# One load of L's diagonal blocks, or four: a change to how the inversion in a gated delta rule layer is fed

## The chip, the cores and the metric

The kernel runs on one core of one Trainium2 chip. The metric is device time in microseconds (us), the median of several executions. Before the change it is 2826.01 us, the median of three runs (2831.53, 2826.01, 2823.58).

## The reference, cut to what matters

Two pre-norm residual layers are computed on 256 tokens of width 2048, in float32. The first mixes tokens by stick-breaking attention, the second by a gated delta rule; each is followed by a SwiGLU feed-forward part. What the change touches is in the second layer, where for each of 32 value heads a lower triangular matrix is inverted:

```
a_mat = where(strict, einsum('nbhcd,nbhsd->nbhcs', k * beta, k) * decay, 0)
t_mat = triangular_solve(a_mat + eye, eye, lower=True, unit_diagonal=True)
u = t_mat @ (v * beta)
w = t_mat @ (k * beta * exp(g))
```

The kernel works with chunks of 128 tokens where the reference has 64, and calls the strictly triangular matrix L.

## The kernel before, in words

**The main stream.** Nearly all the work is products of the 256 tokens with weight matrices, cut into blocks of 512 output columns (`Block`). The weights come from HBM in loads of two row tiles of 128 rows (`load`, 512 KB, the tile `raw`, five buffers; a `qk` block of the delta rule takes two loads of 256 KB for one such tile). `convert` splits each into two float32r parts: ScalarE writes `wh` by a copy (the helper `act`, L190), VectorE writes `wl` by a subtraction (the helper `tt`, L194). TensorE then does 12 products per piece into `acc` (the helper `mm`, L213). Conversions run three pieces ahead (`AHEAD`), and there are four buffers for each of the two parts.

**The side chains.** Everything else (norms, attention, the delta rule) is written as Python generators that the program steps through while it emits the main products. So the order of the instructions on every engine is fixed when the program is built. It is decided by a small model: `self.t` holds a clock for each engine and one for the DMA, `spend` and `transfer` add a cost to them, and `tick` lets a chain go on once its `ready` time has come on the model's TensorE clock and the modelled ScalarE and VectorE clocks are at most `LAG` ahead of it. `transfer` gives each DMA 0.46 us on the issuing queue, then 1.55 us until data flows, its bytes at 360 KB per us, and 0.55 us to land; all DMAs of the model share one line. The DMA clock starts at 0.

**The inversion.** The 32 heads come in eight groups of four. For each group, `gdn_blocks32` writes the 32 x 32 diagonal blocks of L of the four heads and two chunks to a scratch of 32 rows by 1024 in DRAM (eight small DMAs, `scratch<-wide`), and loads the scratch into the tile `lt`, 128 partitions of 4 KB: each quarter of 32 partitions gets the same 128 KB. GpSimd sets the diagonal of `lt` to one (L1003). After that VectorE does 32 steps of forward substitution, two instructions each (`slab<-slab,lt`, L194, and a reduction, L209). The generator yields after some of the steps (`CUT`), so that weight conversions stand between them in VectorE's order. The results go back to a second scratch, and `gdn_inverse` doubles the blocks up to 128 x 128 with products on TensorE.

**Queues.** All these DMAs are issued by SyncE, in program order: a weight load behind the load of `lt` is issued after it. VectorE too executes in order: where an instruction of the substitution waits for `lt`, the conversions behind it wait as well, and TensorE waits for those once it has used up the weights converted ahead.

Of the kernel before, what the change touches and what calls it, by code (L numbers as in the profile page):

```python
# [32 lines left out]
class Slots:  # L33
    """A fixed set of buffers handed out in turn."""
# [13 lines left out]
class Task:  # L48
    """A chain of work that runs between the main matrix products. It yields where its next
    instructions need what it has issued so far; `ready` is when that should be there."""  # L50
# [17 lines left out]
class Operand:  # L68
    """A stationary operand: 128 rows of the contraction for 256 tokens, split into two float32r parts."""
# [8 lines left out]
class Block:  # L78
    """An output block of up to 512 columns: its weights, its stationary operands and what follows it."""
# [8 lines left out]
class Trunk:  # L88
# [10 lines left out]
    LAG = 2.0  # L99
    REST = 8.0  # L100
    GDN_ORDER = [('qk', 0), ('ba',), ('v', 0), ('qk', 1), ('z', 0), ('v', 2), ('v', 1), ('z', 1), ('qk', 2), ('qk', 3), ('v', 3), ('z', 2), ('z', 3), ('out', 0, 4), ('out', 4, 8), ('qk', 4), ('v', 4), ('qk', 5), ('v', 5), ('z', 5), ('z', 4), ('qk', 7), ('v', 6), ('qk', 6), ('out', 8, 16), ('v', 7), ('z', 6), ('z', 7), ('out', 16, 24), ('out', 24, 32)]

    def __init__(self, ctx, tc, ins, out):
        self.tc, self.nc, self.ins, self.out = tc, tc.nc, ins, out
        self.tasks = []
        self.cur = None
        self.table = None
        self.t = {"pe": 0.0, "act": 0.0, "dve": 0.0, "sp": 0.0, "dma": 0.0}
        self.flags = set()
        self.smalls = {}  # L110
        self.persist = ctx.enter_context(tc.tile_pool(name="persist", bufs=1))
        self.wpool = ctx.enter_context(tc.tile_pool(name="weights", bufs=1))
        self.ppool = ctx.enter_context(tc.tile_pool(name="psum", bufs=1, space=PSUM))
        t = self.sb
        self.xs = [t(f"x{n}", [P, NT, NB]) for n in range(4)]
        self.x = [[self.xs[n][:, i, :] for n in range(4)] for i in range(NT)]
        self.hT = []
        for k in range(KT // 2):
            hi, lo = t(f"hTh{k}", [P, 2, S], F32R), t(f"hTl{k}", [P, 2, S], F32R)
            self.hT += [(hi[:, j, :], lo[:, j, :]) for j in range(2)]  # L120
        self.pairs = Slots([(t(f"kh{k}", [P, 2, S], F32R), t(f"kl{k}", [P, 2, S], F32R)) for k in range(self.PAIRS)])
        self.lts = Slots([t("lt", [P, 32, 32])])
        self.slabs = Slots([t(f"slab{k}", [P, NB]) for k in range(self.SLAB)])
        self.gms = Slots([[t(f"gm{k}{hl}", [P, NB], F32R) for hl in range(2)] for k in range(1)])
        self.wide = Slots([t(f"wide{k}", [P, 2, 4, P]) for k in range(self.WIDE)])
        self.acc = [[self.ppool.tile([P, NB], F32, name=f"acc{b}{i}") for i in range(NT)] for b in range(2)]
        self.banks = Slots([self.ppool.tile([P, NB], F32, name=f"bank{k}") for k in range(4)])
        dram = ctx.enter_context(tc.tile_pool(name="scratch", bufs=1, space=bass.MemoryType.DRAM))
        self.scratch = [dram.tile(s, F32, name=f"scratch{k}") for k, s in enumerate(([32, 1024], [8, P * (P + 1)]))]
        self.n = 0  # L130
# [20 lines left out]
    def tick(self, idle=False):  # L151
        """Let the chains go on whose results should be there."""
        ran = False
        for task in list(self.tasks):
            now = self.t["pe"]
            if task.ready <= now and max(self.t["act"], self.t["dve"]) <= now + self.LAG:
                before = dict(self.t)
                self.step(task)
                ran = ran or task.done or before != self.t
        if idle and not ran:  # L160
            later = [task.ready for task in self.tasks if task.ready > self.t["pe"]]
            self.t["pe"] = min(later) if later else self.t["pe"] + 0.1
# [75 lines left out]
    def split(self, hi, lo, src, gain=None):  # L238
        """hi + lo == src (times a gain per partition)."""
        if gain is None:  # L240
            self.act(hi, src)
            self.tt(lo, src, hi.bitcast(F32), ALU.subtract)
        else:
            self.act(hi, src, scale=gain)
            self.stt(lo, src, gain, hi.bitcast(F32), ALU.mult, ALU.subtract)
# [5 lines left out]
    def rsqrt(self, out, in_, scale, eps):  # L251
        """(in * scale + eps) ** -0.5, in place allowed."""
        self.ts(out, in_, scale, ALU.mult, eps, ALU.add)
        self.sync()
        self.act(out, out, AF.Ln)
        self.act(out, out, AF.Exp, scale=-0.5)

# [6 lines left out]
    def constants(self):  # L264
        """What the first products need: the identity and the gains of the mixers' norms, a column to 128 channels."""
        t = self.sb
        self.nc.scalar.preload_act_table_set("natural_log_exp_and_others")
        self.table = 6
        self.ident = t("ident", [P, P])
        self.gains = t("gains", [P, 67])  # L270
        rows = self.slabs.free[0][:32, :P]
        self.nc.scalar.dma_start(rows, self.ins["mix_norm"].rearrange("l (k p) -> (l k) p", p=P))
        make_identity(self.nc, self.ident)
        bank = self.banks.free[0]
        self.tr(bank[:, 0:32], rows)
        self.nc.vector.tensor_copy(self.gains[:, 0:32], bank[:, 0:32])

    def more_constants(self):
        """The other vectors and the masks."""
# [65 lines left out]
    def plan(self, blocks):  # L345
        """Cut blocks into loads of four row tiles and pieces of two."""
# [97 lines left out]
    def load_x(self, n):  # L444
        """Columns n*512.. of x, and the first norm of them."""
# [13 lines left out]
    def norm_begin(self, gain0):  # L459
        """State of one normalisation of x: partial sums and the 16 operands."""  # L460
# [13 lines left out]
    def norm_part(self, st, n):  # L474
        """Transpose columns n*512.. of x into operands."""
# [17 lines left out]
    def norm_stats(self, st, n):  # L493
        """Sum the squares of columns n*512.. of x; the last part gives the scale of each token."""
# [15 lines left out]
        # one Newton step: r * (1.5 - 0.5 * v * r * r)  # L510
# [22 lines left out]
    def pair_operands(self, ops, src, gain=None):  # L533
        """Fill two operands from a [128, 2, 256] source in PSUM."""
# [13 lines left out]
    def transposed_pairs(self, tok, ops, gain=None):  # L548
        """tok: two [128 tokens, 512] slabs -> four operands."""
# [215 lines left out]
    def gdn_gates(self, acc, free):  # L765
        """g = -exp(a_log) * softplus(a + dt_bias), beta = sigmoid(b), per token and head."""
# [42 lines left out]
        # exp of the sum of g over the tokens of chunk 0 after j  # L809
# [15 lines left out]
    def conv(self, jobs):  # L825
        """Causal depthwise convolution over the 256 tokens of channel tiles: (source, result, channel tile)."""
# [31 lines left out]
    def gdn_decay(self, G):  # L858
        """E[j, head, i] = exp of the sum of g over tokens after j up to i: within chunk 0, across, within chunk 1;
        across without the tokens of chunk 0, whose share is in `rest`. For i < j, where nothing looks, it is 1."""  # L860
# [23 lines left out]
    def small(self, name, shape, g):  # L884
        """A small tile, one per three groups in turn."""
        key = (name, g % 3)
        if key not in self.smalls:
            self.smalls[key] = self.sb(f"{name}{g % 3}", shape)
        return self.smalls[key]

    def gdn_scores(self, G):
# [8 lines left out]
        # products of keys with keys and queries: [key token, (k, q), token]  # L900
        m = []
        for j in range(3):
# [10 lines left out]
            # queries see no later keys of their chunk; where L is zero nothing is read  # L913
# [3 lines left out]
        # sums of squares of k and q per token: [token, key head, (k, q), chunk]  # L917
# [29 lines left out]
        # beta / (|k|^2 + eps) and sqrt(|k|^2 + eps)  # L947
# [31 lines left out]
    def gdn_blocks32(self, G):  # L979
        """Inverses of the 32 x 32 diagonal blocks of I + L by forward substitution: partition q * 32 + r holds  # L980
        columns 4q.. and 16 + 4q.. of block r of the eight matrices, and all of the block of L."""
# [18 lines left out]
        self.dma(ltf, bass.AP(tensor=src.tensor, offset=src.offset, ap=[[0, 4], [1024, 32], [1, 1024]]))  # L1000
        yield
        # the diagonal takes the right hand side, which waits negated where the unknown goes
        g.memset(ltf[:, 0:1024:33], 1.0)  # L1003
        for i in range(32):
            n = i + 1
            if i < 16:
                # row i of the left columns and row 16 + i of the right ones
# [23 lines left out]
    def strided(self, a, off, *dims):  # L1031
        """Elements of a [partitions, n] from off on, by (stride, count) per dimension."""
        return bass.AP(tensor=a.tensor, offset=a.offset + off, ap=[list(a.ap[0])] + [[s, n] for s, n in dims])

    def whole(self):
        """Scratch 1 as [128, 8 matrices, 128]."""
        return self.scratch[1][:, :P * P].rearrange("h (j i) -> j h i", i=P)

    def diag(self, at):
        """Rows at.. at + 4 of the 32 x 32 diagonal blocks of the 8 matrices of scratch 1: [32, 4, 32]."""  # L1040
# [3 lines left out]
    def gdn_inverse(self, G, c, a, U):  # L1044
        """U = transpose of (I + L)^-1 for the four heads, by doubling diagonal blocks."""
# [5 lines left out]
        # all but its 32 x 32 diagonal blocks is zero yet: transposed block by block it is transposed  # L1051
# [184 lines left out]
```

## Time and profile before

| | before |
|---|---|
| median of three timed runs | 2826.01 us (2823.58 to 2831.53) |
| span of the profiled execution | 2824.8 us |
| TensorE products busy | 2796.1 us (99% of the span) |
| VectorE busy | 1660.5 us (59%) |
| ScalarE busy | 1363.1 us (48%) |
| GpSimd busy | 11.2 us |
| loads of `lt` | 8, of 512 KB each |

The profile gives no time for the profiled execution beside its span. The stages follow each other in time: attention from 0 to about 420 us, the first feed-forward part to about 1163, the delta rule to about 2063, the second feed-forward part to the end. Products are pipelined and their ends are modelled, so the distance from the start of one to the start of the next says how fast TensorE works; a busy share alone does not.

### The profile page before, as it was taken

How to read it: one execution, taken by the hardware profiler on the slowest of the kernel's cores; microseconds unless marked ns; L12 is line 12 of the kernel's file. 1: busy time of each engine (PE TensorE's matmuls, PEld its weight loads, DVE VectorE, ACT ScalarE, POOL GpSimd, SP SyncE). 2: the span in 40 equal slices, each digit the busy share in tenths (PEclk: the TensorE clock that was granted, in tenths of full speed). 3: DMA queues.
4: the chain of work that ended last, by engine and by line, in shares of the span. 5: the costliest groups of instructions: out<-in, count | busy, mean ns of one | idle time of the engine just before them, and what ended most of it. 6: DMA issues, size and time to landing. Idle time of an engine off the chain costs nothing.

```text
span 2824.8 us, 35294 instructions
## 1 busy us (share of the span) xinstructions
PE 2796.1 (99%) x13290; PEld 2258.6 (80%) x13290; DVE 1660.5 (59%) x2498; ACT 1363.1 (48%) x1896; POOL 11.2 (0%) x95
## 2 busy tenths in 40 slices
PE   8999999999999999999999999999999999999999
PEld 6888888888888888887787788777888888888887
DVE  5555565554454545578777787877654544544544
ACT  5555454434434444565565556545554344344343
POOL 0000000000000000000000000000000000000000
PEclk9999999999999999999999999999999999999999
DMA  6555556566566566555656555545466566566564
GB/s 218 164 160 161 179 165 184 182 191 185 182 188 185 184 187 186 177 165 161 176 145 184 150 158 166 166 140 177 157 181 184 186 185 187 186 185 186 184 186 155
DMA packets 299334, 496.38 MB, mean 176 GB/s; under 512 B 36695, under 2 KB 79002, under 8 KB 299162
## 3 DMA queue, kind: packets, MB, share of 16 engines
q1 hardware_dynamic: 299114, 494.10, 58.0%
q8 instruction: 104, 1.70, 0.3%
q14 instruction: 68, 0.56, 0.1%
q10 hardware_dynamic: 48, 0.02, 0.0%
HBM read 489.33 MB, written 4.72 MB: 175 GB/s over the span
## 4 chain that ended last, share of the span: by engine, by line
PE 92%; DVE 3%; DMA 3%; ACT 1%; issue 1%; SPq 0%; POOL 0%; POOLq 0%; DVEq 0%; ACTq 0%
PE acc L213 85%; PE bank L213 5%; PE bank L222 2%; DMA lt<-scratch 2%; DVE wl L194 1%; DVE slab L194 1%; DVE slab L198 1%; ACT wh L190 0%; ACT slab L190 0%; DVE slab L209 0%; DVE wide L198 0%; DMA x<-in_x_dram 0%; DVE hTl L198 0%; DMA scratch<-wide 0%; SPq L366 0%
## 5 line engine op out<-in xcount | busy, mean ns | idle before, releaser
L194 DVE TENSOR_TENSOR wl<-raw,wh 128x1024 fp32r<-128x1024 f32 x913 | 1110.4, 1222 | 923.3 <-ACT wh L190 922.2
L190 ACT ACTIVATE wh<-raw 128x1024 fp32r<-128x1024 f32 x913 | 959.6, 1057 | 1016.3 <-PE acc L213 997.9
L213 PE MATMUL acc<-wh,hTh 128*128 128x512 f32 x2560 | 1029.3, 402 | 0.0
L213 PE MATMUL acc<-wl,hTh 128*128 128x512 f32 x2560 | 1014.3, 396 | 9.4 <-DVE wl L194 9.4
L213 PE MATMUL acc<-wh,hTl 128*128 128x512 f32 x2560 | 1013.3, 396 | 0.0
L213 PEld LDWEIGHTS acc<-wl,hTh 128*128 128x128 f32 x2560 | 482.3, 188 | 121.0 <-DVE wl L194 12.6
L213 PEld LDWEIGHTS acc<-wh,hTl 128*128 128x128 f32 x2560 | 481.9, 188 | 116.3 <-DVE hTl L198 0.4
L213 PEld LDWEIGHTS acc<-wh,hTh 128*128 128x128 f32 x2560 | 482.3, 188 | 110.0
L213 PE MATMUL acc<-wh,kh 128*128 128x512 f32 x1088 | 438.0, 403 | 0.0
L213 PE MATMUL acc<-wl,kh 128*128 128x512 f32 x1088 | 431.4, 397 | 4.9 <-DVE wl L194 4.9
L213 PE MATMUL acc<-wh,kl 128*128 128x512 f32 x1088 | 431.1, 396 | 0.0
L213 PEld LDWEIGHTS acc<-wl,kh 128*128 128x128 f32 x1088 | 205.3, 189 | 51.4 <-DVE wl L194 5.4
L213 PEld LDWEIGHTS acc<-wh,kl 128*128 128x128 f32 x1088 | 205.1, 189 | 49.6
L213 PEld LDWEIGHTS acc<-wh,kh 128*128 128x128 f32 x1088 | 205.3, 189 | 46.8
L190 ACT ACTIVATE slab<-bank 32x128 f32<-32x128 f32 (+4 forms) x280 | 108.4, 392 | 152.2 <-PE bank L213 134.5
L194 DVE TENSOR_TENSOR slab<-slab,lt 128x88 f32<-128x88 f32 (+23 forms) x256 | 79.1, 309 | 51.2 <-POOL lt L1003 45.3
L190 ACT ACTIVATE slab<-acc,rstd 128x512 f32<-128x512 f32 x116 | 77.4, 686 | 42.7 <-PE acc L213 42.3
L222 PE MATMUL bank<-ident,slab 128*128 128x128 f32 (+1 forms) x502 | 75.8, 273 | 6.3 <-DMA slab<-in_mix_norm_dram 4.2
L194 DVE TENSOR_TENSOR x<-acc,x 128x512 f32<-128x512 f32 x120 | 76.9, 681 | 8.2 <-PE acc L213 8.2
L222 PEld LDWEIGHTS bank<-ident,slab 128*128 128x128 f32 (+1 forms) x502 | 61.9, 140 | 23.6 <-issue 4.6
L198 DVE SCALAR_TENSOR_TENSOR slab<-bank,cw,slab 128x255 f32<-128x255 f32 (+2 forms) x192 | 77.5, 472 | 3.0 <-ACT slab L190 3.0
L209 DVE TENSOR_REDUCE slab<-slab 128x8 f32<-128x8 f32 (+31 forms) x256 | 61.9, 242 | 8.8
(124 smaller groups left out, 962.3 us busy)
## 6 DMA issues: line engine op xcount, KB each, us to landing
raw<-in_ffn_w_gu_dram SPq DMA_DIRECT2D x352, 512.0 KB, 3.8
raw<-in_ffn_w_down_dram SPq DMA_DIRECT2D x176, 512.0 KB, 4.1
raw<-in_gdn_w_in_dram SPq DMA_DIRECT2D x129, 512.0 KB, 3.8
raw<-in_sb_w_in_dram SPq DMA_DIRECT2D x96, 512.0 KB, 3.9
raw<-in_gdn_w_in_dram SPq DMA_DIRECT2D x128, 256.0 KB, 3.1
raw<-in_gdn_w_out_dram SPq DMA_DIRECT2D x64, 512.0 KB, 4.1
raw<-in_sb_w_out_dram SPq DMA_DIRECT2D x32, 512.0 KB, 3.7
lt<-scratch SPq DMA_DIRECT2D x8, 512.0 KB
```

The lines of the kernel that those rows point to most:

```text
L190: self.nc.scalar.activation(out, in_, func, **kw)
L194: self.nc.vector.tensor_tensor(out, a, b, op=op)
L198: self.nc.vector.scalar_tensor_tensor(out, a, s, b, op0=op0, op1=op1)
L209: self.nc.vector.tensor_reduce(out, in_, axis=AX.X, op=ALU.add, **kw)
L213: self.nc.tensor.matmul(out, lhsT, rhs, start=start, stop=stop, skip_group_check=True)
L222: self.nc.tensor.transpose(out, in_, self.ident[:p, :p])
```

## The change

Two things change; besides them the comments are taken out. First, `lt` is filled by four DMAs, one for each quarter of 32 partitions, whose source is the scratch as it lies. Before, one DMA filled all 128 partitions, from a source whose outermost dimension has four steps of zero length. Second, the model's DMA clock starts at a new constant, `FIRST = 3.5`, so that the model lets the first loads land later.

```diff
     LAG = 2.0
+    FIRST = 3.5
     REST = 8.0
...
-        self.t = {"pe": 0.0, "act": 0.0, "dve": 0.0, "sp": 0.0, "dma": 0.0}
+        self.t = {"pe": 0.0, "act": 0.0, "dve": 0.0, "sp": 0.0, "dma": self.FIRST}
...
         lt = yield from self.lts.get()
         ltf = lt.rearrange("p j i -> p (j i)")
         src = self.scratch[0][:]
-        self.dma(ltf, bass.AP(tensor=src.tensor, offset=src.offset, ap=[[0, 4], [1024, 32], [1, 1024]]))
+        for q in range(4):
+            self.dma(ltf[32 * q:32 * q + 32, :], src)
         yield
```

## Rows read from the trace of the kernel before

**Rows 1.** The page: busy time of TensorE (first line of its part 1, with the other engines), and the shares of the chain that ended last, by line.

```profile
PE 2796.1 (99%) x13290; PEld 2258.6 (80%) x13290; DVE 1660.5 (59%) x2498; ACT 1363.1 (48%) x1896; POOL 11.2 (0%) x95
PE acc L213 85%; PE bank L213 5%; PE bank L222 2%; DMA lt<-scratch 2%; DVE wl L194 1%; DVE slab L194 1%; DVE slab L198 1%; ACT wh L190 0%; ACT slab L190 0%; DVE slab L209 0%; DVE wide L198 0%; DMA x<-in_x_dram 0%; DVE hTl L198 0%; DMA scratch<-wide 0%; SPq L366 0%
```

**Rows 2.** Busy time by stretch: the first 12 us, and the delta rule. Columns: stretch, length, then busy us and instructions of TensorE (PE), its weight loads (PEld), VectorE (DVE), ScalarE (ACT) and GpSimd (POOL), granted TensorE clock, share of the DMA engines, GB/s.

```profile
0.00:12.00 12.00, 3.71 (x16) 3.24 (x17) 2.78 (x5) 3.81 (x6) 2.68 (x14) 1.00 0.81 288
...
1163.00:2063.00 900.00, 885.26 (x4873) 713.48 (x4871) 678.44 (x1505) 509.35 (x902) 8.00 (x80) 0.99 0.56 163
```

**Rows 3.** Waits, of TensorE's products in the stretch of the delta rule (first row) and of the other engines over the whole span: engine and line, what it waited for, us in total, times, longest.

```profile
PE acc L213 <- DVE wl L194: 14.3, 7, 4.9
...
POOL lt L1003 <- DMA lt<-scratch: 332.4, 8, 69.0
...
DVE slab L194 <- POOL lt L1003: 45.3, 7, 8.5
```

**Rows 4.** The chain that ended last, in order of time: the five pieces that are a load of `lt`. Start (its issue), length, what.

```profile
1262.34 11.92 DMA lt<-scratch
...
1345.98 11.88 DMA lt<-scratch
...
1544.37 13.11 DMA lt<-scratch
...
1828.91 12.90 DMA lt<-scratch
...
1924.98 11.76 DMA lt<-scratch
```

**Rows 5.** The timeline around the first load of `lt`: start, length, engine, line, operation, out<-in, and in brackets the engine's idle time before it and what ended that.

```profile
1267.01 1.23 DVE L194 TENSOR_TENSOR wl<-raw,wh 128x1024 fp32r<-128x1024 f32 x1 [0.70 <-ACT wh L190]
...
1274.37 0.16 POOL L1003 MEMSET lt<- 128x32 f32 x1 [68.96 <-DMA lt<-scratch]
1274.57 0.17 DVE L194 TENSOR_TENSOR slab<-slab,lt 128x8 f32<-128x8 f32 x1 [6.34 <-POOL lt L1003]
...
1275.58 1.06 ACT L190 ACTIVATE wh<-raw 128x1024 fp32r<-128x1024 f32 x1 [4.16 <-DMA raw<-in_gdn_w_in_dram]
...
1278.29 2.35 DVE L194 TENSOR_TENSOR wl<-raw,wh 128x1024 fp32r<-128x1024 f32 x2
...
1279.56 0.72 PE L213 MATMUL acc<-wl,hTh 128*128 128x512 f32 x1 [3.41 <-DVE wl L194]
```

**Rows 6.** Three stretches by busy time, columns as in rows 2, each beginning where TensorE starts again after a load of `lt`.

```profile
1279.56:1283.08 3.52, 3.52 (x9) 2.74 (x10) 3.28 (x10) 0.00 (x0) 0.00 (x0) 0.52 0.66 186
1562.88:1566.39 3.51, 3.51 (x8) 2.74 (x9) 3.37 (x8) 0.00 (x0) 0.00 (x0) 0.51 0.56 158
1847.10:1853.11 6.01, 6.01 (x14) 4.75 (x15) 5.77 (x12) 0.92 (x1) 0.00 (x0) 0.50 0.57 182
```

**Rows 7.** The timeline of TensorE after the fourth load, columns as in rows 5: two neighbours within the second stretch of rows 6, two behind it.

```profile
1565.11 0.63 PE L213 MATMUL acc<-wh,hTh 128*128 128x512 f32 x1
1565.54 0.63 PE L213 MATMUL acc<-wl,hTh 128*128 128x512 f32 x1
...
1566.86 0.39 PE L213 MATMUL acc<-wh,hTl 128*128 128x512 f32 x1
1567.09 0.40 PE L213 MATMUL acc<-wh,hTh 128*128 128x512 f32 x1
```

**Rows 8.** The timeline of VectorE at the second, the fifth and the seventh load: the instruction that waited for `lt`, at the second also the one before it.

```profile
1348.44 1.23 DVE L194 TENSOR_TENSOR wl<-raw,wh 128x1024 fp32r<-128x1024 f32 x1
1358.20 0.17 DVE L194 TENSOR_TENSOR slab<-slab,lt 128x8 f32<-128x8 f32 x1 [8.53 <-POOL lt L1003]
...
1655.52 0.17 DVE L194 TENSOR_TENSOR slab<-slab,lt 128x8 f32<-128x8 f32 x1 [1.23 <-POOL lt L1003]
...
1842.11 0.17 DVE L194 TENSOR_TENSOR slab<-slab,lt 128x8 f32<-128x8 f32 x1 [7.91 <-POOL lt L1003]
```

**Rows 9.** DMA packets in three stretches: 1274.4 to 1276 us, after the first load of `lt` has landed; 1263.5 to 1264.5, before most of it moves; 1261.34 to 1278.34. Packets, MB, and the share of the time of 16 engines (rows with "q1"), or the counts by size.

```profile
q1 hardware_dynamic: 84, 0.16, 26.7%
...
q1 hardware_dynamic: 164, 0.33, 90.2%
...
DMA packets 1370, 2.90 MB, mean 170 GB/s; under 512 B 84, under 2 KB 84, under 8 KB 1370
```

**Rows 10.** The page's DMA rows: ScalarE's queue (q10), its only load, and loads on SyncE's queue with KB each and median us from issue to landing.

```profile
q10 hardware_dynamic: 48, 0.02, 0.0%
...
raw<-in_gdn_w_in_dram SPq DMA_DIRECT2D x129, 512.0 KB, 3.8
raw<-in_gdn_w_in_dram SPq DMA_DIRECT2D x128, 256.0 KB, 3.1
...
slab<-in_gdn_conv_w_dram SPq DMA_DIRECT2D x2, 64.0 KB, 3.8
slab<-in_mix_norm_dram ACTq DMA_DIRECT2D x1, 16.0 KB
```

**Rows 11.** The timeline: the load of q10 and the product that waited for it, at the start; and eight issues in a row on SyncE's queue, before the first load of `lt`.

```profile
0.83 0.43 ACTq L272 DMA_DIRECT2D slab<-in_mix_norm_dram  x1
...
4.25 0.28 PE L222 MATMUL bank<-ident,slab 32*128 32x32 f32 x1 [4.25 <-DMA slab<-in_mix_norm_dram]
...
1251.75 5.16 SPq L226 DMA_DIRECT2D scratch<-wide  x8
```

## The prediction, made blind

> **What bounds the kernel now.** I read the page first: TensorE's products are busy for 2796.1 of 2824.8 us, so at most 28.7 us of idle time can be won without making the products themselves faster. The chain that ended last names one thing besides arithmetic that has a share worth a look: the load of `lt`, 2% [rows 1]. Next I cut the span into stages. The first 12 us have 8.3 us of idle TensorE, the delta rule 14.74 (900 less 885.26) [rows 2]; that is 23 of the 28.7. Waits tell whose it is: in the delta rule, 14.3 us, seven times, are waits of a product for `wl` from VectorE [rows 3]. VectorE is busy only 678 of those 900 us [rows 2], so it isn't full; it stands. It waited 45.3 us, seven times, for GpSimd's write to `lt`, and GpSimd for the load [rows 3]. The chain shows five of the eight loads on the path, 11.8 to 13.1 us each [rows 4].
>
> The first load is the example to follow in the timeline. It is issued at 1262.34 [rows 4]; VectorE ends its last conversion at 1268.24 and stands for 6.34 us; GpSimd's write runs at 1274.37, 12.03 after the issue. VectorE then does eight steps of the substitution before the next conversion at 1278.29, and TensorE, out of converted weights, has stood for 3.41 us. A weight load queued behind it is late as well: ScalarE waits 4.16 us for `raw` [rows 5].
>
> There is a second price. [...] Products start 0.43 us apart there and 0.23 apart behind it [rows 7]. The three stretches hold 9 + 8 + 14 = 31 products [rows 6], so they lose 31 x 0.20 = 6.2 us. Idle time and clock together: 14.3 + 6.2 = 20.5 us is what late loads of `lt` cost, if all of it is theirs.
>
> **Why the load is slow.** The size isn't it: weight loads of the same 512 KB land in 3.8 us at the median [rows 10]. The packets show what is. Just after the load was issued the 16 DMA engines were 90.2% busy; from 1274.4 to 1276, when `lt` is there and only weight loads issued behind it are under way, 26.7% [rows 9], about four engines out of 16 still working off a backlog. So the transfer sits on a quarter of the engines, and holds up every load's share on those. The small packets agree: 84 under 512 B in the stretch is 5 x 16 + 4 [rows 9], as if each weight load ended with 16 of them and this one with four.
>
> **Part 1, the four loads.** Each fills 32 partitions from 32 plain rows. The nearest row is the load of `mix_norm`: 32 rows, 48 packets on its own queue [rows 10], 32 of data and 16 others, so by the same count all 16 engines. It was issued at 0.83 and its reader ran at 4.25 [rows 11], 3.4 us. I expect the same spread for the four.
>
> Cost on SyncE: eight issues in a row took 5.16 us, 0.65 each [rows 11]; three more are 1.9 us per group, and 24 more over the kernel. Weight loads queued behind leave 1.9 us later, against the 4.16 us by which one was late before [rows 5] on the engines that are now relieved; five buffers of about 2.8 us of products each (12 x 0.23) [rows 7] cover that. If they didn't, it would cost 1.9 us at up to eight places, 15 us.
>
> Landing: the last of four is issued 1.9 us after the first, takes 3.4 for its way [rows 11] and some 0.5 more for 128 KB in place of 16 (a quarter of 512 KB at the 332 GB/s of 0.33 MB in 1 us [rows 9] is 0.4): 5.8 us. The bounds: 3.8 us if four behave as one weight load, and 12.4 if each takes the 3.1 us of a 256 KB load [rows 10] and none begins before the other has ended. I take 5.8, since eight neighbours on this queue were issued at that pace without waiting for each other.
>
> [...]
>
> The wait that remains: GpSimd's write now waits for four transfers in place of one; behind it on GpSimd stand only the memsets of the next group. VectorE waits for it at the same place in its order, and the conversions are queued behind. VectorE arrives 3.7 us after the issue at the second load (1349.67 less 1345.98), where its pause was the longest, and 5.9 after it at the first [rows 4, 5, 8]; with 5.8 and the 0.2 us from GpSimd's start to VectorE's [rows 5] the pauses are 2.3 us in place of 8.53, and 0.1 in place of 6.34. TensorE survives that: a pause of 6.34 us cost 3.41 [rows 5], one of 7.91 cost 4.9 [rows 3, 8], so about 3 us are always covered by weights converted ahead, and the pause of 1.23 [rows 8] cost nothing. So the 14.3 us go, and with the pauses the low clock after them. It takes little: each us by which the load comes earlier is a us off every pause, so 5 us would do.
>
> What is late next: I see nothing that steps in. VectorE gets back some 40 us of its time, and the weight loads are no longer held up on four engines.
>
> **Part 2, the model's clocks.** `FIRST` moves the model's first landing from 0.11 + 1.55 + 1.46 + 0.55 to 3.5 + 1.46 + 0.55, 1.84 us later, and the other eight first loads by as much, since they follow each other on the model's line. All that `tick` compares are differences of clocks that hang on these landings, so I count on the same order of instructions and no change on the chip. If the order did change, the stake is a part of the 8.3 idle us of the first 12 [rows 2]: 2 us either way.
>
> The four loads change the model too: one load is ready 3.71 us after its issue there, four 3.99 (three issues of 0.46 more, a quarter of the bytes at the end). From the first inversion on, the order of instructions of the delta rule can differ by a step here and there. I price that at zero, from -2 us to a new pause of the size of the worst one: 4.9 idle and 14 slow products (2.8), 7.7 us [rows 3, 6].
>
> **Sum.** 2824.8 - 14.3 - 6.2 = 2804.3 for the profiled execution. The median of the runs lies 1.2 above its span, so 2805.5; with half a us for what small pauses leave, 2806.
>
> **Rivals.**
> *Slower: the source is the bottleneck.* Four copies are read from the same 128 KB of DRAM. If that limits the load to what it had, the four end 1.9 us later than the one, at 13.9. The place is VectorE's wait, the point from which it decides is a landing of 12.0: beyond it all seven pauses grow by 1.9, the six long ones reach TensorE, 11 us, and two or three more pauses bring the slow clock, 8 x 0.20 = 1.6 each. Time: 2826 + 11 + 4 = 2841. For it: no other load repeats a source. Against it: the backlog after the landing is of weight loads, whose source doesn't repeat, and it runs on a quarter of the engines too.
> *No change: the four go one after another,* 12.4 us as in the upper bound. For it: the load of 64 KB takes as long as one of 512 [rows 10], so most of a load's time is not data. Against it: SyncE's queue had eight issued in 5.16 us. Time: 2826 to 2829. [...]
> *Less faster: a new pause.* The order of instructions changes and one pause of 7.7 us arises: 2814. For it: VectorE is 75% busy there; against: only waits for `lt` have been long.
>
> **Chances.** My forecast 0.76, a new pause 0.12, one after another 0.07, the source 0.05. About 0.3%, 8.5 us, is what a measurement of this kernel can tell from no change. Faster by more than that: 0.76 + 0.11 = 0.87; within: 0.08; slower: 0.05. The forecast itself spans 2802 to 2809; the range goes to the new pause and some noise of the median: 2801 to 2817.
>
> **What would show it.** Right: GpSimd's write to `lt` 5 to 7 us after the first issue; VectorE's wait for it under 10 us in total; no wait of TensorE for `wl` over 1 us; granted clock 1.00 through the delta rule; the start as before to 1250 us. Wrong: a landing beyond 9 us, or waits for `wl` at other places.

## The result, and the profile after

The changed kernel takes 2804.01 us (four runs, 2803.97 to 2804.02), the kernel before 2826.2 on the same occasion (four runs, 2823.58 to 2831.53). The ratio is 0.992, with a 95% interval of 0.9908 to 0.9933: 22 us less, against 20 forecast, and inside the range of 2801 to 2817. The profiled execution has a span of 2802.3 us in place of 2824.8.

The page of the kernel after: the chain that ended last, by engine and by line (for [rows 1]), and the row of the new loads.

```profile
PE 98%; ACT 1%; DVE 1%; DMA 0%; issue 0%; SPq 0%; ACTq 0%
PE acc L214 90%; PE bank L214 5%; PE bank L223 2%; ACT slab L191 0%; ACT wh L191 0%; DMA x<-in_x_dram 0%; DVE wl L195 0%; DVE hTl L199 0%; ACT hTh L191 0%; DVE slab L195 0%; DVE x L195 0%; DVE sbsq L210 0%; SPq L367 0%; SPq L447 0%; ACT sbsq L191 0%
...
lt<-scratch SPq DMA_DIRECT2D x32, 128.0 KB, 5.0
```

The load of `lt` is gone from the chain, which is now TensorE's for 98%. The loads land 5.0 us after their issue at the median. Lines stand one or two further down than before: L214 is the helper of the products, L195 that of `wl`, L1005 GpSimd's write to `lt`.

Busy time in the stretch of the delta rule, for the last of [rows 2], with the same columns:

```profile
1163.00:2063.00 900.00, 899.68 (x4972) 727.96 (x4971) 693.00 (x1528) 524.03 (x926) 7.99 (x80) 1.00 0.56 167
```

TensorE is busy 899.68 of 900 us where it was 885.26, and the granted clock is 1.00 where it was 0.99. The waits, for [rows 3]; the first row is the only wait of a product in that stretch:

```profile
PE bank L223 <- ACT slab L191: 0.2, 1, 0.2
...
POOL lt L1005 <- DMA lt<-scratch: 296.1, 8, 62.8
...
DVE slab L195 <- POOL lt L1005: 15.4, 5, 3.9
```

No product waits for `wl` any more. VectorE still waits for `lt`, 15.4 us in place of 45.3, and no pause is longer than 3.9. The timeline around the first load, for [rows 5]:

```profile
1262.19 1.74 SPq L227 DMA_DIRECT2D lt<-scratch  x4
...
1266.86 1.23 DVE L195 TENSOR_TENSOR wl<-raw,wh 128x1024 fp32r<-128x1024 f32 x1 [0.71 <-ACT wh L191]
...
1267.95 0.16 POOL L1005 MEMSET lt<- 128x32 f32 x1 [62.78 <-DMA lt<-scratch]
1268.14 0.17 DVE L195 TENSOR_TENSOR slab<-slab,lt 128x8 f32<-128x8 f32 x1
```

GpSimd writes 5.76 us after the first issue, where it was 12.03, and VectorE goes from the conversion to the substitution without a pause. At the fourth group it looks less good:

```profile
1536.65 0.41 SPq L227 DMA_DIRECT2D lt<-scratch  x1
...
1546.46 0.16 POOL L1005 MEMSET lt<- 128x32 f32 x1 [49.47 <-DMA lt<-scratch]
1546.65 0.17 DVE L195 TENSOR_TENSOR slab<-slab,lt 128x8 f32<-128x8 f32 x1 [3.88 <-POOL lt L1005]
```

There the load takes 9.81 us. The DMA packets of that time (1536.65 to 1546.46; packets, MB, share of the time of 16 engines) show that it isn't alone:

```profile
q1 hardware_dynamic: 2610, 2.69, 104.5%
```

The engines are full: besides the 0.52 MB of `lt` they move over 2 MB of weight loads and of the loads issued just before. That isn't the whole reason for the 9.81 us, as the run y_rows below shows. TensorE doesn't notice this either.

**Where the 22 us lie.** In both programs every engine has the same instructions in the same order, but for the split load. So the same event can be looked up in both traces, and the lead of the new kernel over the old read off. The issue of `lt` is such an event: at the first group 1262.34 before [rows 4] and 1262.19 after, a lead of 0.15; at the second 1345.98 and 1340.91, 5.07; at the seventh 1828.91 and 1815.75, 13.16; at the eighth 1924.98 and 1903.92, 21.06; at the end 22.5. From the seventh to the eighth alone, where the product waited 4.9 us and 14 ran at a granted clock of 0.50 [rows 6], 7.9 are won.

### The profile page after: what moved, and what is told of

Read it like the earlier page. It is cut to its first block, busy times and chain, and to the rows that moved or that the text cites. A ratio compares the mean times of both kernels' runs of the same rounds, so it can differ in the third digit from the quotient of the medians.

```text
span 2802.3 us, 35341 instructions
## 1 busy us (share of the span) xinstructions
PE 2788.1 (99%) x13290; PEld 2254.9 (80%) x13290; DVE 1661.0 (59%) x2498; ACT 1363.8 (49%) x1896; POOL 11.2 (0%) x95
## 4 chain that ended last, share of the span: by engine, by line
PE 98%; ACT 1%; DVE 1%; DMA 0%; issue 0%; SPq 0%; ACTq 0%
PE acc L214 90%; PE bank L214 5%; PE bank L223 2%; ACT slab L191 0%; ACT wh L191 0%; DMA x<-in_x_dram 0%; DVE wl L195 0%; DVE hTl L199 0%; ACT hTh L191 0%; DVE slab L195 0%; DVE x L195 0%; DVE sbsq L210 0%; SPq L367 0%; SPq L447 0%; ACT sbsq L191 0%
## 5 line engine op out<-in xcount | busy, mean ns | idle before, releaser
L195 DVE TENSOR_TENSOR wl<-raw,wh 128x1024 fp32r<-128x1024 f32 x913 | 1110.8, 1223 | 925.8 <-ACT wh L191 922.0
L214 PE MATMUL acc<-wh,hTh 128*128 128x512 f32 x2560 | 1028.4, 402 | 0.0
L214 PE MATMUL acc<-wl,hTh 128*128 128x512 f32 x2560 | 1012.2, 395 | 0.0
L214 PE MATMUL acc<-wh,hTl 128*128 128x512 f32 x2560 | 1012.1, 395 | 0.0
L214 PEld LDWEIGHTS acc<-wh,hTl 128*128 128x128 f32 x2560 | 481.0, 188 | 116.4 <-DVE hTl L199 0.3
L214 PEld LDWEIGHTS acc<-wh,hTh 128*128 128x128 f32 x2560 | 481.5, 188 | 109.9
L214 PEld LDWEIGHTS acc<-wl,hTh 128*128 128x128 f32 x2560 | 481.6, 188 | 108.6 <-DVE wl L195 0.3
L214 PE MATMUL acc<-wh,kh 128*128 128x512 f32 x1088 | 437.0, 402 | 0.0
L214 PE MATMUL acc<-wl,kh 128*128 128x512 f32 x1088 | 430.1, 395 | 0.0
L214 PE MATMUL acc<-wh,kl 128*128 128x512 f32 x1088 | 430.0, 395 | 0.0
L214 PEld LDWEIGHTS acc<-wh,kl 128*128 128x128 f32 x1088 | 204.4, 188 | 49.5
L214 PEld LDWEIGHTS acc<-wh,kh 128*128 128x128 f32 x1088 | 204.5, 188 | 46.6
L214 PEld LDWEIGHTS acc<-wl,kh 128*128 128x128 f32 x1088 | 204.6, 188 | 45.9
L195 DVE TENSOR_TENSOR slab<-slab,lt 128x88 f32<-128x88 f32 (+23 forms) x256 | 79.2, 309 | 21.4 <-POOL lt L1005 15.4
L195 DVE TENSOR_TENSOR x<-acc,x 128x512 f32<-128x512 f32 x120 | 77.0, 682 | 8.2 <-PE acc L214 8.2
```

What stands on the lines that cost most here:

```text
L195: self.nc.vector.tensor_tensor(out, a, b, op=op)
L214: self.nc.tensor.matmul(out, lhsT, rhs, start=start, stop=stop, skip_group_check=True)
```

## The experiments

Time is the median; "write" is the time from the first issue to GpSimd's write to `lt`, least to most over the eight groups; the waits are those of VectorE for `lt` and of products for `wl`, in total, us.

| kernel | loads per group | write | VectorE waits | products wait | time |
|---|---|---|---|---|---|
| before | 1, outermost dimension 4, repeated | 10.5 to 13.3 | 45.3 | 14.3 | 2826.2 |
| after | 4 of 32 partitions | 5.8 to 9.8 | 15.4 | 0 | 2804.0 |
| x_first_only | as before | 9.8 to 13.6 | 45.9 | 15.6 | 2827.9 |
| x_gap | 1, outermost dimension 4, not repeated | 10.9 to 13.4 | 48.6 | 17.1 | 2826.3 |
| x_plain | 1 of 128 partitions | 4.6 to 7.1 | 6.2 | 0 | 2804.3 |
| x_two | 2 of 64, outermost dimension 2 | 15.7 to 17.0 | 77.9 | 42.9 | 2866.2 |
| y_rows | 4 of 32, no row read twice | 5.9 to 9.7 | 14.8 | 0 | 2804.0 |
| y_eight | 8 of 32, half the columns | 5.8 to 8.5 | 13.3 | 0 | 2805.1 |
| y_sixteen | 16 of 32, a quarter of the columns | 8.7 to 12.6 | 31.6 | 3.0 | 2813.3 |

y_rows was executed once, the others several times. Writes and waits are read from the one profiled execution of each kernel, which took 2833.1 us in x_gap and 2810.9 in y_sixteen, the slowest and nearly the fastest of theirs; the time beside them is the median. In all of them every engine but SyncE, which issues the loads, has the same instructions in the same order as before. The diffs are against the changed kernel; `FIRST` stays in all.

**x_first_only: which part of the change is it?**

```diff
-        for q in range(4):
-            self.dma(ltf[32 * q:32 * q + 32, :], src)
+        self.dma(ltf, bass.AP(tensor=src.tensor, offset=src.offset, ap=[[0, 4], [1024, 32], [1, 1024]]))
```

> FIRST = 3.5 alone, with the one load as before. My theory: the model's clocks shift together, the order of instructions on every engine stays as before, so 2826 us within the spread of before (2823 to 2832), TensorE's waits for wl in the delta rule about 14 us. Rival (the model's later first landings take part in the gain): under 2820 us, with a start or a delta rule that differs from before.

2827.88 us over ten runs (2823.57 to 2833.41), a ratio of 1.0009 to before (0.9999 to 1.0018). The built program has the same instructions in the same order as before on every engine. The new constant does nothing, and all of the gain is the load's.

**x_gap: the outermost dimension or the repeated source?**

```diff
-        self.scratch = [dram.tile(s, F32, name=f"scratch{k}") for k, s in enumerate(([32, 1024], [8, P * (P + 1)]))]
+        self.scratch = [dram.tile(s, F32, name=f"scratch{k}") for k, s in enumerate(([132, 1024], [8, P * (P + 1)]))]
...
+            self.dma(self.scratch[0][32:132, 512 * c:512 * c + 512], s[:100, :])
...
-        blocks = self.scratch[0][:].rearrange("r (j i) -> r j i", j=32)
+        blocks = self.scratch[0][:32].rearrange("r (j i) -> r j i", j=32)
...
-        for q in range(4):
-            self.dma(ltf[32 * q:32 * q + 32, :], src)
+        self.dma(ltf, bass.AP(tensor=src.tensor, offset=src.offset, ap=[[33 * 1024, 4], [1024, 32], [1, 1024]]))
```

> One load again, its source still with an outermost dimension of four, but no byte is read twice: the scratch has 132 rows, the four steps are 33 rows apart. (Rows 32 to 131 hold zeros, so three quarters of lt have no L: those columns of the inverses are left out.) Theory, the outermost four puts the load on four DMA engines: landing 10 to 13 us after the issue as before, VectorE's wait for lt about 45 us, time 2820 to 2832. Rival, the repeated source is the bottleneck: landing 4 to 6 us, no wait of TensorE, time 2802 to 2808.

2826.26 us, ratio 1.0002 (0.9992 to 1.0011); the write comes 10.9 to 13.4 us after the issue. No row is read twice, and nothing is better. This is the rival of the slower case, and it falls: the source isn't what limits. The DMA packets just after the first landing (1276 to 1277 us), for the first of [rows 9]:

```profile
q1 hardware_dynamic: 50, 0.10, 25.6%
```

Again only weight loads are left, and they keep a quarter of the 16 engines busy.

**x_two: half as many engines.**

```diff
-        for q in range(4):
-            self.dma(ltf[32 * q:32 * q + 32, :], src)
+        for q in range(2):
+            self.dma(ltf[64 * q:64 * q + 64, :], bass.AP(tensor=src.tensor, offset=src.offset, ap=[[0, 2], [1024, 32], [1, 1024]]))
```

> Two loads of 64 partitions, each with a source that repeats twice. Theory, the outermost dimension sets the number of engines, so both are on two engines: 64 packets of 4 KB on each where the one load had 32, landing 17 to 22 us, each of the eight waits of VectorE 6 to 9 us longer than before, time 2870 to 2900. Rival, only the repeat by four or the size of one transfer matters, and two halves share the work: landing 6 to 9 us, time 2804 to 2812.

2866.17 us, ratio 1.0143 (1.0128 to 1.0158): two loads are slower than one. The direction is the theory's and the rival is out, but the size is a little short of it: a write after 15.7 to 17.0 us where I gave 17 to 22, and a time just under the 2870 to 2900. After the first landing (1280 to 1282) the packets say how many engines it was:

```profile
q1 hardware_dynamic: 50, 0.10, 12.6%
```

Two of 16 are 12.5%, four are 25%. So the loads with an outermost dimension of four ran on about four engines, by the 26.7% of [rows 9] and the 25.6% of x_gap, and both loads of x_two on the same two, by the 12.6%.

**x_plain: four loads or one plain one.** The scratch is that of x_gap.

```diff
-        for q in range(4):
-            self.dma(ltf[32 * q:32 * q + 32, :], src)
+        self.dma(ltf, self.scratch[0][:P])
```

> One plain load of 128 rows of a scratch of 132, no row read twice, the order of everything else as before. (Rows 32 to 127 hold zeros, so three quarters of lt have no L, as in the run before.) Theory, all 16 engines take part and the four loads only pay for three more issues: landing 4 to 5 us where nothing else is under way, 1.3 us sooner than the last of four; where weight loads fill the engines (the fourth and the last group) still 7 to 9. TensorE doesn't wait in either, so the time is that of the changed kernel, 2803 to 2805. [...]

2804.28 us, as the changed kernel. The time is as expected, the landing only in part: in the quiet first group 4.96 us against 5.76, but in the fourth 6.13 against 9.81, where I had expected 7 to 9. Over the groups the plain load lands 0.7 to 3.7 us sooner, so loads of 32 partitions that are slower by over 2 us in every group don't fit either. That it ran on all 16 engines is an estimate from the small packets: the whole run has 36811 under 512 B and that of x_gap 36715, and the 96 between are 8 x 16 less 8 x 4, as if a load ended with one on each of its engines. The timeline of the fourth group, x_plain:

```profile
1537.53 0.42 SPq L227 DMA_DIRECT2D lt<-scratch  x1
...
1543.66 0.16 POOL L1005 MEMSET lt<- 128x32 f32 x1 [46.41 <-DMA lt<-scratch]
```

**y_rows: why are four slower than one where the engines are full?**

```diff
-            self.dma(ltf[32 * q:32 * q + 32, :], src)
+            self.dma(ltf[32 * q:32 * q + 32, :], self.scratch[0][32 * q:32 * q + 32])
```

> Four loads of 32 partitions as in the changed kernel, but each from its own 32 rows of a scratch of 132, so that no row is read twice. (Rows 32 to 127 hold zeros, so three quarters of lt have no L.) The one plain load landed 1.2 us sooner than four at the median of the groups and 3.7 sooner in the fourth. Theory A, four copies of the same rows slow the reads: now GpSimd's writes come 4.9 to 7.5 us after the first issue, the fourth group under 8, VectorE's wait for lt 8 us or less. Theory B, loads of 32 partitions are slow by themselves: 5.8 to 9.8 us as in the changed kernel, fourth group 9 or more, VectorE's wait 13 to 18 us. In both TensorE waits for nothing, 2804 us.

5.9 to 9.7 us, the fourth group 9.2, VectorE's wait 14.8: theory B's numbers. Reading the same rows four times costs nothing here (5.8 to 9.8 in the changed kernel). The landing alone doesn't show that the loads of 32 partitions are slow in themselves, since part of their delay is the 1.3 us between the first issue and the last. The packets do show it. In each group exactly 128 packets are of 4 KB, the rows of `lt`. In the changed kernel such a packet takes 229 to 308 ns (medians of the eight groups), in y_rows 219 to 321, in x_plain 159 in every group. The engines are as busy in either case, but they move less. In the fourth group, while `lt` is under way, the changed kernel (1540.15 to 1543.15) and x_plain (1541 to 1543), columns as for the first of [rows 9]:

```profile
q1 hardware_dynamic: 391, 0.68, 110.3%
...
q1 hardware_dynamic: 366, 0.73, 101.7%
```

That is 0.68 MB in 3 us against 0.73 in 2. So full engines alone don't make the 9.81 us, for x_plain meets them too. Why a packet takes longer with four loads of 32 partitions stays open; no time hangs on it.

**y_eight and y_sixteen: how much delay does TensorE bear?**

```diff
         for q in range(4):
-            self.dma(ltf[32 * q:32 * q + 32, :], src)
+            for c in range(0, 1024, 512):
+                self.nc.sync.dma_start(ltf[32 * q:32 * q + 32, c:c + 512], src[:, c:c + 512])
+            self.cur.ends("dma", self.transfer(P * 1024, self.cur.begins("dma")))
```

For y_sixteen 256 stands for 512.

> The four loads cut in two along the columns, eight of 64 KB, order of everything else and the model's prices as in the changed kernel. Theory, only landing counts and TensorE is covered for about 3 us: four more issues of 0.45 us make it 7.5 to 11.5 us, VectorE waits 25 to 32 us in total and at most 6 at once, TensorE loses 0 to 2 us in all: 2804 to 2807 us. Rival, each issue costs in itself (weight loads behind on SyncE's queue come late): 32 more issues cost 0.45 us each, 2814 us or more.

> The four loads cut in four along the columns, 16 of 32 KB, order and prices as in the changed kernel. Theory, only landing counts: twelve more issues of 0.45 us, landing 11 to 15 us, VectorE waits 45 to 60 us in total, TensorE loses as in the kernel before or somewhat more, 14 to 22 us idle and 6 to 9 by the low clock: 2824 to 2836 us. Rival, what matters is the hold on four of the engines, which delays weight loads too, and not the landing: with all 16 engines in use TensorE loses under 5 us, 2804 to 2810.

y_eight takes 2805.12 us (2804.29 to 2806.03): 32 more issues cost 1.1 us at most. But it isn't the test of slack that I meant, since the eight landed no later than the four. y_sixteen takes 2813.34 (2809.62 to 2816.45), between the two expectations. I had put its landing at 11 to 15 us; the small loads land 2.2 us after their issue at the median, so it was 8.7 to 12.6. By the small packets as in x_plain they ran on all 16 engines, an estimate: 38711 under 512 B in the whole run, 36695 before, and the 2016 between are 128 x 16 less 8 x 4. What it gives is pauses between those of after and before. The timelines show, for the seventh group, VectorE's pause and the wait of the next product in three kernels. Before (the pause is in [rows 8]):

```profile
1847.10 0.79 PE L213 MATMUL acc<-wl,kh 128*128 128x512 f32 x1 [4.93 <-DVE wl L194]
```

x_two:

```profile
1878.69 0.17 DVE L195 TENSOR_TENSOR slab<-slab,lt 128x8 f32<-128x8 f32 x1 [10.77 <-POOL lt L1005]
...
1883.67 0.79 PE L214 MATMUL acc<-wl,kh 128*128 128x512 f32 x1 [7.80 <-DVE wl L195]
```

y_sixteen:

```profile
1830.64 0.17 DVE L195 TENSOR_TENSOR slab<-slab,lt 128x8 f32<-128x8 f32 x1 [4.30 <-POOL lt L1007]
...
1835.67 0.50 PE L214 MATMUL acc<-wl,kh 128*128 128x512 f32 x1 [1.36 <-DVE wl L195]
```

Pause less wait: 7.91 - 4.93 = 2.98, 10.77 - 7.80 = 2.97, 4.30 - 1.36 = 2.94. The cover, the part of a pause that TensorE doesn't feel, is a property of the place, and beyond it TensorE loses microsecond for microsecond. The fourth group has another cover, and the same agreement. The timeline of x_two there:

```profile
1578.64 0.17 DVE L195 TENSOR_TENSOR slab<-slab,lt 128x8 f32<-128x8 f32 x1 [10.91 <-POOL lt L1005]
...
1583.68 0.80 PE L214 MATMUL acc<-wl,hTh 128*128 128x512 f32 x1 [5.54 <-DVE wl L195]
```

And that of y_sixteen:

```profile
1549.86 0.17 DVE L195 TENSOR_TENSOR slab<-slab,lt 128x8 f32<-128x8 f32 x1 [6.80 <-POOL lt L1007]
...
1554.90 0.50 PE L214 MATMUL acc<-wl,hTh 128*128 128x512 f32 x1 [1.43 <-DVE wl L195]
```

10.91 - 5.54 = 5.37 and 6.80 - 1.43 = 5.37. The smallest cover is at the third group, where only x_two has a pause:

```profile
1470.11 0.18 DVE L195 TENSOR_TENSOR slab<-slab,lt 128x8 f32<-128x8 f32 x1 [4.39 <-POOL lt L1005]
...
1475.10 0.79 PE L214 MATMUL acc<-wl,hTh 128*128 128x512 f32 x1 [3.05 <-DVE wl L195]
```

4.39 - 3.05 = 1.34.

That the cover is the same in three kernels settles y_sixteen's rival as well: with two, four or 16 engines in use the same pause costs the same, so it is the landing that counts and not the hold on four engines. The weight load that came late before [rows 5] cost nothing of its own: at that group pause less wait is 6.34 - 3.41 = 2.93, and in x_two, where ScalarE waits 0.3 us for `raw` and not 4.16, it is 11.26 - 8.33 = 2.93 as well.

## Why the prediction was right, point by point

- **What bounds the kernel** (late loads of `lt`, through VectorE's order, to TensorE): right. With the load early, the idle time in its stretch falls from 14.74 to 0.32 us; with it later still, 42.9 us of waits arise (x_two).
- **Why the load is slow** (a quarter of the engines): right, by x_gap (25.6%) and x_two (12.6%). That this also delays the weight loads behind it was seen rightly, but it cost no time.
- **Landing, 5.8 us:** the mis-sized term. The write came 5.8 to 9.8 us after the first issue, in five groups of eight within the 5 to 7 that I gave, in the fourth and the eighth (9.81 and 9.14) beyond the 9 that I had called a sign of being wrong. That the first group hit 5.8 is partly luck: the three further issues took 1.31 us and not 1.9, and from the last issue to the write it was 4.45 and not 3.9. The data was sized too small. I gave the last load's 128 KB 0.5 us; the packets of `lt` start over 2.5 us in the first group and over 5.5 in the eighth, since with four loads of 32 partitions each takes longer (229 to 308 ns against 159 in x_plain, under y_rows) and other loads stand between them. The bounds of 3.8 and 12.4 held. VectorE's wait came to 15.4 us where I had written under 10, and VectorE got back 29.9 us and not some 40.
- **The cover of TensorE, about 3 us:** right as a mechanism and for the two places that it was read from, 2.93 at the first group and 2.98 at the seventh. But "always" was wrong: the cover is 5.37 at the fourth, 1.34 at the third and 2.46 at the fifth (6.93 less 4.47 in x_two). The wrong landing cost nothing all the same, since the changed kernel has no pause at the third and the fifth, and elsewhere its pauses stay below the cover of their place (3.88 at the fourth, 1.26 at the seventh).
- **The sum, 20.5 us:** 22.5 were won in the span. The 6.2 for the clock stand for 31 products that start 0.20 us further apart at a granted clock of 0.50 to 0.52 [rows 6, 7]; after the change that clock is 1.00 over the delta rule. Part of the difference is in how idle time is shown: it counts from a product's modelled end, about 0.40 us after its start, while the next could start after 0.23 [rows 7]. So each of seven waits was 0.17 longer than its row says, 1.2 us together. Another 0.15 was won before the first load. The rest, about 0.6, I can't put down to a row. The time around the span is 1.7 us, where I took 1.2. That half us is made up by the half us that I had kept for small pauses, so the 22 in place of 20 is the span's.
- **Part 2, the model's clocks:** `FIRST` changes nothing, as forecast (x_first_only). That the four loads' price in the model could move other instructions was a needless fear: not one did, so the rival of a new pause had no ground.
- **The rivals:** the slower case fell with x_gap and y_rows; one after another fell with the first group's 5.76 us. One load in place of four lands sooner where it is plain (x_plain, 4.6 to 7.1 us against 5.8 to 9.8), and later with an outermost dimension of four (x_gap, 10.9 to 13.4).

## What to carry to other kernels

Look at a slow load's outermost dimension before its size: here it decided on how many of the 16 DMA engines 512 KB ran (25.6% busy at four, 12.6% at two), and four plain transfers, or one of 128 plain rows, brought them in about half the time (5.8 to 9.8 and 4.6 to 7.1 us against 10.5 to 13.3). (x_plain leaves three of the four copies out; what it would cost to write them to the scratch wasn't measured.) What a late load costs is read at the engine that bounds: the pause of the waiting engine less a cover that belongs to the place (1.34 to 5.37 us here), plus what the lower clock costs where it falls after the stop. It did so after three of the seven waits before (0.50 to 0.52, [rows 6]), and after neither wait of 1.4 us in y_sixteen, where products start 0.23 us apart soon after (1555.24 and 1555.47, 1836.01 and 1836.24). With all pauses below their cover, an even faster load (x_plain, 2804.3 us against 2804.0) was worth nothing.

## What the runs showed that I had not expected

The spread of the runs went with the waits: 2823.58 to 2831.53 before, 0.05 us in all after. Why the late load makes it uneven isn't shown; in y_sixteen, with an estimated 16 engines in use, the time spread as well, from 2809.62 to 2816.45.

And the granted clock fell without a stop. In y_eight, busy time by stretch, columns as in [rows 2]:

```profile
1603.40:1606.80 3.40, 3.40 (x46) 2.76 (x46) 3.40 (x5) 1.54 (x3) 0.00 (x0) 1.00 0.43 129
1606.80:1610.20 3.40, 3.40 (x11) 2.51 (x10) 1.18 (x10) 3.27 (x8) 0.00 (x0) 0.50 0.60 183
```

TensorE is shown as busy in both, but in the second the clock is at 0.50, and the products into `acc` start 0.43 us apart (1606.96 and 1607.39) where it was 0.23 (1605.26 and 1605.49). Around them (1600 to 1611) its products by group are, besides those into `acc`, mostly small ones. Columns as on the page: operands, count, busy us and mean ns, idle us before.

```profile
L214 PE MATMUL bank<-slab,wide 32*32 32x32 f32 x32 | 1.2, 194 | 0.0
L214 PE MATMUL bank<-negones,slab 128*128 128x1 f32 x8 | 1.1, 253 | 0.0
```

All 40 of these stand in the first of the two stretches. y_eight's span is 1.6 us longer than that of the changed kernel (2803.9 and 2802.3), with no wait for `wl` in it; product by product, all of it arises in this stretch. It wasn't a single event. At the same place of the program the profiled executions of y_sixteen and x_gap lost the clock too, again with TensorE shown as busy, 3.40 of 3.40 us; theirs:

```profile
1609.80:1613.20 3.40, 3.40 (x10) 2.58 (x9) 1.11 (x10) 3.27 (x8) 0.00 (x0) 0.50 0.41 106
...
1621.00:1624.40 3.40, 3.40 (x9) 2.65 (x9) 1.41 (x10) 3.24 (x9) 0.00 (x0) 0.50 0.52 145
```

So an estimated 1.6, by y_eight, of the 6.9 us by which y_sixteen's span is longer than the changed kernel's have nothing to do with a wait for `lt`. Before and after run the same products in the same order at a clock of 1.00 there (before 1612 to 1622.2, after 1598 to 1611.6), and x_plain and y_rows have a mean of 1.000 over the whole run, so the small products alone don't decide. That they have a part in it is a guess of mine; no run tests it. What is shown is that a busy share of 100% doesn't exclude a clock of 0.50.
